# A block of stick-breaking attention beside a gated delta rule: the attention product with its scores as weights, fewer chains of reciprocal roots, and another order of projections and output

## The chip, the cores and the metric

One core of one Trainium2 chip runs the whole kernel in one launch. The metric is the device time of one execution in microseconds; it was taken three times for the kernel before, with a median of 704.29.

## What is computed

The reference is one decoder block on a sequence of 1024 tokens of width 1024. After an RMS norm, one input projection gives queries, keys, values and a gate for each of two groups of heads. Eight heads of 64 do strictly causal stick-breaking attention, four heads of 128 a gated delta rule in chunks. Each group is normed per head and gated with silu, both halves together go through the output projection, and the residual is added and normed.

```python
proj = jnp.einsum('btd,de->bte', h, w_in[layer])
sb_q, sb_k, sb_v, sb_z, g_q, g_k, g_v, g_z, g_b, g_a = jnp.split(proj, split_idx, axis=-1)
o_sb = stick_breaking_attention(...)   # A[t,s] = sigmoid(z_ts) * prod_{s<j<t} (1 - sigmoid(z_tj)); o = A v
o_sb = rmsnorm(o_sb.transpose(0, 2, 1, 3), sb_norm_w[layer]).reshape(b, t_len, SB_WIDTH) * jax.nn.silu(sb_z)
qkv = jax.nn.silu(causal_depthwise_conv(jnp.concatenate([g_q, g_k, g_v], axis=-1), gdn_conv_w[layer]))
gq, gk = l2norm(...), l2norm(...)
o_gdn = gated_delta_chunked(gq, gk, gv, decay, beta)   # S_t = exp(g) S (I - beta k k^T) + beta k v^T; o = S^T q
o_gdn = rmsnorm(o_gdn.transpose(0, 2, 1, 3), gdn_norm_w[layer]).reshape(b, t_len, GDN_WIDTH) * jax.nn.silu(g_z)
x = x + jnp.einsum('bte,ed->btd', jnp.concatenate([o_sb, o_gdn], axis=-1), w_out[layer])
return rmsnorm(x, final_norm_w)
```

## The kernel before

**Numbers in two parts.** The large products run in fp32r. An operand is split into a high part that fp32r holds and a low part, the rest; `mm3` (lines 514 to 517) makes a product of three matmuls from the two parts of each side. The scores of attention are split the same way into `ah` and `al`, while the values are kept with their high and low part side by side in `v2` (128 columns for a head of 64).

**Order.** The kernel does not fix its order by hand. Every piece of work is a generator (a `Stream`), and a model of the five engines (`Model`, lines 138 to 300) plays the program while it is recorded: an operation starts when its inputs are there by the model's costs, the streams take turns by priority, and the order that comes out is pinned on each engine as it stands. On TensorE the order is that in which the streams emit. One number of the model is how long TensorE needs at least between the starts of two matmuls, for the load of the weights (`op.columns`, line 169, used in line 285). The list `ORDER` (line 29) sets the order of the projections: `v0`, `v1` are the halves of the attention's values, `k0` to `k3` its keys, `z0` to `z7` the eight column blocks of the gates, `G0` to `G3` the query, key and value of a delta head. The projections are the filling: they go in where no other stream has work for TensorE (priority 100).

**Attention.** `window` (line 1125) treats two query blocks of 128 tokens at a time, so a head has four windows `w`. For each block, TensorE makes the logits in `z` (bank `pz`), ScalarE two sigmoids, VectorE the running product from the right (`cc`, a scan), Pool the product of both into `sg`. Then, in steps `j`, TensorE transposes the score blocks, ScalarE rounds them to `ah`, VectorE subtracts for `al`, and lines 1181 to 1185 multiply: the stationary operand (the weights) is the block `v2[:, s, :]`, the moving one `ah` or `al` with the columns of both query blocks, 256, or 128 where the key block is the last. The result `ov` (bank `po`) is transposed, so ScalarE copies it to `o2`, TensorE transposes that twice, VectorE adds the high and the low half in `oe`, and a DMA stores it in `o_s`. At most `WINDOWS` = 3 windows are in flight.

**Delta rule.** A head has two halves `g` of four chunks of 128 tokens. `gdn_pre` (line 879) transposes keys and queries, squares them with a sum, and runs a chain of a reciprocal root by Newton steps on VectorE (`_rsqrt`, 10 instructions on 8 numbers a row) for each of the eight halves; `gdn_inv` inverts the triangular matrices by blocks; `gdn_chain` runs the recurrence and ends with another such chain on 4 numbers a row (lines 1085 to 1091).

**Output.** `mixed` loads block `b` of 128 tokens of both groups from DRAM and norms it; `prepare` transposes it, applies the gates and splits it into `mh` and `ml`; `product` does 48 matmuls of 512 columns a block with the weights of the output projection, in the order of the eight row blocks `k`: 0 to 3 belong to attention, 4 to 7 to the delta rule. `out_weights` loads and splits those rows (`wo_split`: ScalarE makes `woh`, VectorE `wol`), 0 to 3 when the delta rule has ended, 4 to 7 when the projections have ended, since their place is that of the projections' input.

Of the kernel before, what the change touches and what calls it, by code (L numbers as in the profile page):

```python
# [10 lines left out]
F32 = mybir.dt.float32  # L11
# [6 lines left out]
P = 128  # L18
# [10 lines left out]
ORDER = "v0 v1 G0 k0 G1 z0 G2 k1 G3 k2 z1 z2 k3 z3 z4 z5 z6 z7".split()  # L29
WINDOWS = 3  # L30
# [72 lines left out]
class Pool:  # L103
# [6 lines left out]
    def tile(self, shape, dtype, name, tag=None, bufs=1):  # L110
# [7 lines left out]
        if len(slots) == bufs:  # L118
            old = next((r for r in slots if r.idle(self.ck.now)), slots[0])
            slots.remove(old)  # L120
            before += old.ops
# [16 lines left out]
class Model:  # L138
# [141 lines left out]
    def pull(self):  # L280
        if self.pe and not self.pe_busy and not self.pe[0].waits:
# [3 lines left out]
            at = max(self.now, op.ready, self.pe_began + 0.834 * op.columns)  # L285
# [107 lines left out]
def interleave(ck, room, streams):  # L393

    while streams:
        now = []
        if not ck.pe:
            free = room()
            now = [s for s in streams if (free or s.prio >= 100) and s.ready(ck)]
# [23 lines left out]
def block(tc, xT_d, x_d, n1_d, wE_d, wQ_d, wC_d, conv_d, alog_d, dtb_d, mixw_d, wo_d, fnw_d, out_d):  # L423
# [4 lines left out]
    with ExitStack() as top:  # L428
# [36 lines left out]
        rsg = cst.tile([P, GH, NB], F32, name="rsg")  # L465
        gsc = {n: cst.tile([P, GH, NB], F32, name=n) for n in ("beta", "cum", "eg", "neg", "egl", "kd")}
# [5 lines left out]
        o_s = dr.tile([NB, P, 512], F32, name="o_s")  # L472
# [55 lines left out]
        for tag, bufs in (("kh", 1), ("kl", 1), ("q2", 1), ("v2a", 2), ("v2a", 2), ("cc", 2), ("cc", 2), ("sg3", 1)):  # L528
            chl.append(at_.tile([P, 2, 520], F32R, tag=tag, bufs=bufs, name="chl"))
        sm = at_.tile([P, 768], F32, tag="sg2", name="sm")  # L530
# [95 lines left out]
        busy = {"w0": 0, "w1": 0, "w2": 0, "w3": 0, "T": 0, "al": 0, "po": 0, "inv": 0}  # L626
# [3 lines left out]
        def values(part):  # L630
            cs = slice(264 * part, 264 + 256 * part)
            n = 264 - 8 * part
            for b in range(NB):
                if part == 0 and 4 < b < 7:
                    row_scale(b - 5, dgs)
                if part == 0 and 4 <= b < 6:
                    dgp = at_.tile([P, 2, 256], F32, tag="sg0", name="dg")
                    dgs = [diagonal(dgp, 2 * (b - 4) + g) for g in range(2)]
# [16 lines left out]
        def decays(me):  # L655
# [41 lines left out]
            for h in range(GH):  # L697
                for g in range(2):
                    hc = slice(4 * g, 4 * g + 4)
                    dt = gd.tile([P, 4, P], F32, tag=("kn", "at", "nkv")[(2 * h + g) % 3], bufs=3, name="dt")  # L700
# [27 lines left out]
        def z_evac(i):  # L728
            def evac(pt, half):
# [9 lines left out]
                return S.dma_start(gate_s[i, :, hs], zt)  # L739
# [37 lines left out]
        def projections():  # L777
# [8 lines left out]
            def take():  # L786
                for n, (name, ok) in enumerate(todo):
                    if ok():
# [4 lines left out]
                        e = 4 + 4 * int(name[2]) + int(name[1]) if name[0] == "G" else e + int(name[1])  # L793
# [57 lines left out]
        def delta_pre():  # L851
            yield lambda: "v0" in flags
            yield from decays(pre)
            for h in range(GH):
                for g in range(2):
# [13 lines left out]
        def delta_scan():  # L869
            for h in range(GH):  # L870
                for g in range(2):
# [4 lines left out]
                    flags[f"c{u}"] = True  # L876
            flags["g"] = True

        def gdn_pre(h, g):
            st = gst[h, g] = {}  # L880
            kq, vt = gst[h]["kq"][g], gst[h]["vt"]
            cs = slice(4 * g, 4 * g + 4)
            kn = gd.tile([P, 4, P], F32, tag="kn", bufs=3, name="kn")
            ss = gd.tile([P, 2, 4], F32, tag="ss", name="ss")
# [4 lines left out]

            nkv = gd.tile([P, 4, P], F32, tag="nkv", bufs=3, name="nkv")  # L890
            for which in range(2):
                tp = pz()
                for j in range(4):
                    TE.transpose(tp[:, j * P:(j + 1) * P], kq[:, j, which, :], ident)
                for j in range(4):
                    A.activation(nkv[:, j, :], tp[:, j * P:(j + 1) * P], AF.Square, accum_out=ss[:, which, j:j + 1])
                sq = [("A", 250)] * 4
                if which == 0:
                    V.tensor_copy(kn.rearrange("p c d -> p (c d)"), tp)
                    yield  # L900
            V.tensor_scalar(ss, ss, EPS, None, ALU.add)
            rr = gd.tile([P, 2, 4], F32, tag="rr", bufs=3, name="rr")
            _rsqrt(V, gd, rr.rearrange("p a c -> p (a c)"), ss.rearrange("p a c -> p (a c)"), 8, "rru")
            r2b = gd.tile([P, 4], F32, tag="r2b", bufs=3, name="r2b")
            V.tensor_tensor(r2b, rr[:, 0, :], rr[:, 0, :], ALU.mult)
            V.tensor_tensor(r2b, r2b, gsc["beta"][:, h, cs], ALU.mult)
            mr2b = gd.tile([P, 4], F32, tag="mr2b", name="mr2b")
            r = V.tensor_scalar(mr2b, r2b, -1.0, None, ALU.mult)
            nk = gd.tile([P, 4], F32, tag="nk", name="nk")
            V.tensor_tensor(nk, ss[:, 0, :], rr[:, 0, :], ALU.mult)  # L910
            r2k = gd.tile([P, 4], F32, tag="r2k", bufs=3, name="r2k")
            V.tensor_tensor(r2k, r2b, gsc["kd"][:, h, cs], ALU.mult)
            yield r
            nm = dt
            at = gd.tile([P, 4, P], F32, tag="at", bufs=3, name="at")
# [12 lines left out]
            st.update(kn=kn, rr=rr, r2b=r2b, r2k=r2k, nkv=nkv, nm=nm, at=at)  # L928
# [10 lines left out]
        def gdn_inv(h, g):  # L939
# [45 lines left out]
            V.tensor_copy(W[0:32, :, 0:32], wc[0:32])  # L985
            V.tensor_copy(W[32:64, :, 32:64], wc[32:64])
# [24 lines left out]
            for q in range(2):  # L1011
                o = 64 * q
                V.tensor_copy(X[o:o + 32, :, o + 32:o + 64], xv[o:o + 32])
# [16 lines left out]
        def gdn_chain(h, g):  # L1030
            st = gst[h, g]
            kq, kn, nkv, at = gst[h]["kq"][g], st["kn"], st["nkv"], st["at"]
            r2b, r2k, rr = st["r2b"], st["r2k"], st["rr"]
# [369 lines left out]
```

## Time and profile before

| | |
|---|---|
| Time, median of 3 runs (lowest to highest) | 704.29 us (703.46 to 705.93) |
| The profiled execution, its own time | 705.37 us |
| Its span in the profile | 703.7 us |
| Granted TensorE clock, mean | 0.989 |
| DMA | 96.42 MB, 137 GB/s on average |

The profile's page has the busy time of each engine (PE is TensorE, PEld its weight loads, DVE VectorE, ACT ScalarE, POOL GpSimd, SP the queue of the DMAs), the span in slices, and the chain of work that ended last: from the last instruction back to what released it, step by step. The groups gather instructions of one kind; since every operation is recorded through one helper, all have the line L315, and groups are told apart by the tiles that they write and read (`po<-ah,v2a` writes `po` and reads `ah` and `v2a`). A duration in the groups runs from an instruction's start to its end; matmuls overlap, so the step from start to start is shorter.

### The profile page before, as it was taken

Reading aid. Unit: us, or ns where it says so; the run is one execution under the profiler, and the core shown is the slowest. Engines: PE = TensorE matmul, PEld = TensorE weight load, DVE = VectorE, ACT = ScalarE, POOL = GpSimd, SP = SyncE. Lnnn points to the kernel's source line nnn. Section 1 sums busy time; section 2 is a strip of 40 time slices with the busy share of each in tenths; the row PEclk is TensorE's granted clock in tenths of the full one; section 3 lists DMA queues with packets and bytes.
Section 4 is the critical chain, followed back from the end, with each engine's and each line's share of the span. In section 5 each row is a group of like instructions: output and inputs, shape, how many; then the busy total and the mean of one; then the engine's idle time right before and its main releaser. Section 6 shows DMA issues by size and latency. Waiting matters only on the chain.

```text
span 703.7 us, 12998 instructions
## 1 busy us (share of the span) xinstructions
PE 680.7 (97%) x4510; PEld 575.7 (82%) x4510; DVE 544.7 (77%) x1463; ACT 363.4 (52%) x885; POOL 263.9 (38%) x223
## 2 busy tenths in 40 slices
PE   8999999999899999999999999999999999889995
PEld 6889998887677888878888888888788888678885
DVE  5364525668898987898999999897787987997843
ACT  5661248436567543675856677643377853311212
POOL 0000147545352523442344442454335455443221
PEclk9999999999899999999999999999999999999998
DMA  8936364271142236224235051333524366645321
GB/s 300 370 121 255 112 223 162 90 260 32 49 139 75 69 97 206 71 70 141 72 109 169 12 173 42 109 96 105 174 65 153 98 225 225 217 145 181 113 94 61
DMA packets 76498, 96.42 MB, mean 137 GB/s; under 512 B 24656, under 2 KB 45712, under 8 KB 76432
## 3 DMA queue, kind: packets, MB, share of 16 engines
q1 hardware_dynamic: 76432, 95.58, 42.1%
q8 instruction: 36, 0.59, 0.4%
q14 instruction: 30, 0.25, 0.1%
HBM read 67.67 MB, written 27.89 MB: 136 GB/s over the span
## 4 chain that ended last, share of the span: by engine, by line
PE 86%; DVE 7%; issue 2%; ACT 2%; DMA 1%; SPq 0%; POOLq 0%; POOL 0%; DVEq 0%
PE pp L315 55%; PE pz L315 23%; PE po L315 5%; PE pc L315 3%; DVE cc L315 2%; DMA xr<-xT 1%; DVE pp L315 1%; ACT sg L315 1%; DVE y L315 0%; DVE al L315 0%; ACT pz L315 0%; DVE tm L315 0%; DVE wol L315 0%; DMA xc<-xd 0%; ACT xinv L315 0%
## 5 line engine op out<-in xcount | busy, mean ns | idle before, releaser
L315 PE MATMUL pp<-xh,weh 128*128 128x512 f32 x384 | 161.0, 419 | 0.5 <-DVE ac L315 0.5
L315 PE MATMUL pp<-xh,wel 128*128 128x512 f32 x384 | 151.2, 394 | 0.0
L315 PE MATMUL pp<-xl,weh 128*128 128x512 f32 x384 | 150.7, 393 | 0.0
L315 POOL TENSOR_TENSOR sg<-sg,cc 128x128 f32<-128x128 f32 (+3 forms) x64 | 77.3, 1209 | 114.7 <-DVE cc L315 74.5
L315 POOL TENSOR_TENSOR wel<-wer,weh 128x512 fp32r<-128x512 f32 x48 | 62.9, 1313 | 85.2 <-ACT weh L315 82.3
L315 PEld LDWEIGHTS pp<-xh,wel 128*128 128x128 f32 x384 | 72.4, 188 | 16.2
L315 PEld LDWEIGHTS pp<-xh,weh 128*128 128x128 f32 x384 | 72.6, 189 | 12.3 <-DVE ac L315 1.1
L315 PEld LDWEIGHTS pp<-xl,weh 128*128 128x128 f32 x384 | 72.8, 190 | 10.2
L315 ACT ACTIVATE sg<-pz,rs 128x384 f32<-128x384 f32 (+3 forms) x96 | 53.1, 586 | 18.5 <-PE pz L315 17.8
L315 ACT ACTIVATE ah<-pz 128x512 fp32r<-128x512 f32 (+1 forms) x80 | 43.7, 558 | 29.6 <-PE pz L315 28.8
L315 DVE TENSOR_TENSOR_SCAN cc<-pz,step 128x384 f32<-128x384 f32 (+2 forms) x64 | 53.9, 847 | 2.8 <-ACT pz L315 2.4
L315 PE MATMUL pp<-wol,mh 128*128 128x512 f32 (+1 forms) x136 | 52.1, 383 | 1.3 <-DVE wol L315 1.3
L315 DVE TENSOR_TENSOR al<-pz,ah 128x512 fp32r<-128x512 f32 (+1 forms) x80 | 49.9, 629 | 3.6 <-ACT ah L315 3.3
L315 PE MATMUL pp<-woh,mh 128*128 128x512 f32 (+1 forms) x136 | 52.6, 387 | 0.0
L315 PE MATMUL pp<-woh,ml 128*128 128x512 f32 (+1 forms) x136 | 52.0, 382 | 0.6 <-POOL ml L315 0.6
L315 ACT ACTIVATE pz<-pz,ns 128x384 f32<-128x384 f32 (+3 forms) x96 | 52.0, 564 | 0.1
L315 PE MATMUL pz<-step,sg 128*128 128x128 f32 x288 | 45.3, 281 | 3.7 <-DVE oe L315 2.4
L315 PE MATMUL pp<-chl,xh 128*128 128x264 f32 (+1 forms) x256 | 46.8, 284 | 0.0
L315 DVE TENSOR_TENSOR tm<-xs,br 128x8 f32<-128x8 f32 (+14 forms) x120 | 45.0, 375 | 0.9
L315 DVE SCALAR_TENSOR_TENSOR pp<-pre,conv,pp 128x512 f32<-128x512 f32 x48 | 36.0, 751 | 8.7 <-ACT pp L315 8.4
L315 POOL TENSOR_TENSOR ml<-mf,mh 128x512 fp32r<-128x512 f32 x16 | 24.5, 1536 | 48.2 <-ACT mh L315 47.0
L315 PE MATMUL po<-ah,v2a 128*128 128x256 f32 (+1 forms) x160 | 42.3, 288 | 0.0
(234 smaller groups left out, 1613.5 us busy)
## 6 DMA issues: line engine op xcount, KB each, us to landing
wer<-wE SPq DMA_DIRECT2D x48, 256.0 KB, 3.6
xr<-x SPq DMA_DIRECT2D x16, 512.0 KB, 6.2
qk_s<-xq SPq DMA_DIRECT2D x8, 512.0 KB, 4.7
v_s<-v2e SPq DMA_DIRECT2D x16, 256.0 KB, 2.0
q<-qk_s SPq DMA_DIRECT2D x8, 512.0 KB, 4.2
v2a<-v_s SPq DMA_DIRECT2D x8, 512.0 KB, 7.2
kh<-qk_s SPq DMA_DIRECT2D x8, 512.0 KB, 4.6
kl<-qk_s SPq DMA_DIRECT2D x8, 512.0 KB, 6.1
```

The lines of the kernel that those rows point to most:

```text
L315: ins = f(*args, **kw).ins
```

## The change

1. **The attention product.** A window is one query block `b` (eight a head, up to six in flight). The stationary operand is now a 128x128 block of `ah` or `al`, the moving one `v2[:, k, :]`, 128 columns. The result is not transposed; ScalarE copies it from `po` to `oe` and a DMA stores its high and low half apart in `o_s`. The two halves are added by Pool in `mixed`. The copy `o2`, its transposes and the reduction on VectorE go.
2. **The model** takes 0.42 ns a column for the load of fp32r weights and 0.834 for others, where it took 0.834 for all.
3. **Chains.** `gdn_norms` does the norms of both halves of a head at once: four chains on 16 numbers a row instead of eight on 8. The chain at the end of `gdn_chain` becomes one for all heads, on 32 numbers a row, when the last head has ended. The copies into `kn`, `W` and part of `X` move from VectorE to ScalarE.
4. **Projections.** `v1` comes after `k0`, `z1` after `k3`, and the gates are numbered so that `z0` to `z3` are the delta rule's.
5. **Output.** The weight rows 4 to 7 are loaded and split first, during attention. `mixed_delta` prepares the delta rule's half of a block alone, ahead of `mixed`; the product takes the halves in the order (0, delta), (1, delta), (0, attention), (1, attention), and from block 2 on the delta rule's rows first.

```diff
-ORDER = "v0 v1 G0 k0 G1 z0 G2 k1 G3 k2 z1 z2 k3 z3 z4 z5 z6 z7".split()
-WINDOWS = 3
+ORDER = "v0 G0 k0 v1 G1 z0 G2 k1 G3 k2 k3 z1 z2 z3 z4 z5 z6 z7".split()
+WINDOWS = 6
...
-            op.columns = int(np.prod(inputs[0].shape[1:]))
+            op.load = int(np.prod(inputs[0].shape[1:])) * (0.42 if inputs[0].dtype == F32R else 0.834)
...
+        def gdn_norms(h):
+
+            ss = gd.tile([P, 2, NB], F32, tag="ss", name="ss")
...
+                    if which == 0:
+                        A.activation(kns[g].rearrange("p c d -> p (c d)"), tp, AF.Copy)
+
+                    for j in range(4):
+                        js = tp[:, j * P:(j + 1) * P]
+                        A.activation(js, js, AF.Square, accum_out=ss[:, which, 4 * g + j:4 * g + j + 1])
+                    yield
+            V.tensor_scalar(ss, ss, EPS, None, ALU.add)
+            rr = rkq[:, h]
+            _rsqrt(V, gd, rr.rearrange("p a c -> p (a c)"), ss.rearrange("p a c -> p (a c)"), 2 * NB, "rru")
...
-            V.tensor_copy(W[0:32, :, 0:32], wc[0:32])
-            V.tensor_copy(W[32:64, :, 32:64], wc[32:64])
+            A.activation(W[0:32, :, 0:32], wc[0:32], AF.Copy)
+            A.activation(W[32:64, :, 32:64], wc[32:64], AF.Copy)
...
-            _rsqrt(V, gd, t0, sso, 4, "t0u")
-            V.scalar_tensor_tensor(rsg[:, h, 4 * g:4 * g + 4], rq, P ** -0.5, t0, ALU.mult, ALU.mult)
...
-                for s in (2 * (j - 1), 2 * (j - 1) + 1):
-                    i0 = 0 if s <= 2 * w else 1
-                    c = slice(256 * (s % 2), 256 * (s % 2) + (1 if i0 else 2) * P)
-                    for m, t in enumerate((ah, al)):
-                        TE.matmul(ov[:, i0 * P:256], v2[:, s, :], t[:, c], start=(s == 0 and m == 0), stop=(s == 2 * w + 1 and m == 1))
+                for u in range(n):
+                    k = 4 * (j - 1) + u
+                    for t in (ah, al):
+                        TE.matmul(ov, t[:, u * P:(u + 1) * P], v2[:, k, :], start=(k == 0 and t is ah), stop=(k == b and t is al))
...
-            o2 = at_.tile([P, 256], F32, tag="o2", name="o2")
-            yield A.activation(o2, ov[:, 0:256], AF.Copy)
+            oe = at_.tile([P, P], F32, tag="oe", bufs=3, name="oe")
+            yield A.activation(oe, ov, AF.Copy)
             busy["po"] = 0
-            op = pz()
-            for i in range(2):
-                TE.transpose(op[:, i * P:(i + 1) * P], o2[:, i * P:(i + 1) * P], ident)
-            oe = at_.tile([P, 2, SBD], F32, tag="oe", bufs=2, name="oe")
-            V.tensor_reduce(oe, op[:, 0:256].rearrange("p (i u d) -> p i d u", i=2, u=2), AX.X, ALU.add)
-            flags[f"e{h}{w}"] = S.dma_start(o_s[2 * w:2 * w + 2, :, h * SBD:(h + 1) * SBD].rearrange("b t d -> t b d"), oe)
+            flags[f"e{h}{b}"] = S.dma_start(o_s[b, :, :, h * SBD:(h + 1) * SBD].rearrange("u t d -> t u d"), oe.rearrange("p (u d) -> p u d", u=2))
...
-            for k in range(4):
+            for k in range(4, NK):
                 yield wo_raw(k)
                 wo_split(k)
             flags["wo"] = True
...
+                S.dma_start(mx[:, 0:512], o_s[b, 0])
+                sq = fi.tile([P, 512], F32, tag="sq", name="sq")
+                S.dma_start(sq, o_s[b, 1])
+                gate6(b)
+                G.tensor_tensor(mx[:, 0:512], mx[:, 0:512], sq, ALU.add)
+                G.tensor_tensor(sq, mx[:, 0:512], mx[:, 0:512], ALU.mult)
...
+        def halves():
+            return [(0, 1), (1, 1), (0, 0), (1, 0)] + [(b, g) for b in range(2, NB) for g in (1, 0)]
...
+                ks = [4, 5, 6, 7, 0, 1, 2, 3]
+                if b < 2:
+                    ks = ks[0:4] if half else ks[4:8]
```

The same place on TensorE in both orders, an attention product in the middle of a head. `po<-ah,v2a` is a matmul of AV; the size is that of its result (partitions x columns). Before:

```order
L315 MATMUL po<-ah,v2a 128x256
L315 MATMUL po<-al,v2a 128x256
L315 MATMUL po<-ah,v2a 128x128
L315 MATMUL po<-al,v2a 128x128
L315 MATMUL pz<-kh,q_2098 128x512
L315 MATMUL pz<-kl,q_2098 128x512
L315 MATMUL pz<-wc,dt 32x32 x16
L315 MATMUL pz<-step,o_2247 128x128 x2
```

Now, in two pieces, the beginning and the end of one group. `po<-v2a,ah` is a matmul that moves `v2` past a block of `ah`; `pc<-xct` and `pz<-v_2445,kn` are the delta rule's:

```order
L316 MATMUL pp<-xh,weh 128x512
L316 MATMUL pp<-xl,weh 128x512
L316 MATMUL pp<-xh,wel 128x512
L316 MATMUL pc<-xct,xinv_537 128x128
L316 MATMUL po<-v2a,ah 128x128
L316 MATMUL po<-v2a,al 128x128
```

The end of the group, and what follows it on TensorE:

```order
L316 MATMUL po<-v2a,ah 128x128
L316 MATMUL po<-v2a,al 128x128
L316 MATMUL pz<-v_2445,kn 128x128
L316 MATMUL pz<-step,sg 128x128 x4
L316 MATMUL pp<-xh,weh 128x512
```

Between these two pieces the pair of `ah` and `al` repeats: 14 matmuls of 128 columns stand in a row, where two or three wider pairs and one narrow one stood; the transposes of `o` are gone, and the results of AV have 128 columns each.

On VectorE, at the end of the projections. `zt<-pp` is the last gate's evacuation, `wol` the split of a row block of output weights, `mf` the gated half of an output block, `ssb` and `rsb` the norm of the next. Before:

```order
L315 TENSOR_TENSOR zt<-pp,rbc 128x512
L315 SCALAR_TENSOR_TENSOR wol_7646<-wor,mixw,woh_7645 128x1024
L315 SCALAR_TENSOR_TENSOR wol_7650<-wor,mixw,woh_7649 128x1024
L315 TENSOR_TENSOR mf<-pz,gt 128x384
L315 TENSOR_TENSOR mf<-pz,zt 128x128
L315 TENSOR_TENSOR mf<-pz,gt 128x512
L315 TENSOR_REDUCE ssb<-sq 128x8
L315 TENSOR_SCALAR ssb<-ssb 128x8
L315 TENSOR_SCALAR rsb<-ssb 128x8
L315 SCALAR_TENSOR_TENSOR wol_7654<-wor,mixw,woh_7653 128x1024
L315 SCALAR_TENSOR_TENSOR wol_7658<-wor,mixw,woh_7657 128x1024
```

Now:

```order
L316 TENSOR_TENSOR mx<-mx,rsb 128x512
L316 TENSOR_TENSOR zt<-pp,rbc 128x512
L316 TENSOR_TENSOR mf<-pz,gt 128x384
L316 SCALAR_TENSOR_TENSOR wol_7783<-wor,mixw,woh_7782 128x1024
L316 SCALAR_TENSOR_TENSOR wol_7787<-wor,mixw,woh_7786 128x1024
L316 SCALAR_TENSOR_TENSOR wol_7791<-wor,mixw,woh_7790 128x1024
L316 SCALAR_TENSOR_TENSOR wol_7795<-wor,mixw,woh_7794 128x1024
L316 TENSOR_TENSOR mf<-pz,zt 128x128
L316 TENSOR_SCALAR mx<-mx,rsg 128x128 x4
```

The four splits of the last rows stand together, ahead of the last quarter of block 0's attention half (`mf<-pz,zt`); the rows that were split here earlier, 0 to 3 of the old order, are split as 4 to 7 further up, between the scans of attention.

More of the change, by code (lines that the diff above doesn't have):

```diff
@@ L118, in tile @@
         if len(slots) == bufs:
-            old = next((r for r in slots if r.idle(self.ck.now)), slots[0])
+            old = slots[0] if turn else next((r for r in slots if r.idle(self.ck.now)), slots[0])
             slots.remove(old)
@@ L284, in pull @@
             self.begin(op)
-            at = max(self.now, op.ready, self.pe_began + 0.834 * op.columns)
+            at = max(self.now, op.ready, self.pe_began + op.load)
             self.pe_began = at
@@ L398, in interleave @@
             free = room()
-            now = [s for s in streams if (free or s.prio >= 100) and s.ready(ck)]
+            now = [s for s in streams if (free or s.prio >= 100 or s.prio < 0) and s.ready(ck)]
         if not now:
@@ L625, in block @@
         gst = {}
-        busy = {"w0": 0, "w1": 0, "w2": 0, "w3": 0, "T": 0, "al": 0, "po": 0, "inv": 0}
+        busy = {**{f"w{b}": 0 for b in range(NB)}, "T": 0, "al": 0, "po": 0, "inv": 0}
         def values(part):
@@ L888, in gdn_pre @@
             S.dma_start(dt, dt_s[h, g])
[L890 to L913, printed above, removed]
+            nkv = gd.tile([P, 4, P], F32, tag="nkv", bufs=3, turn=True, name="nkv")
             nm = dt
-            at = gd.tile([P, 4, P], F32, tag="at", bufs=3, name="at")
+            at = gd.tile([P, 4, P], F32, tag="at", bufs=3, turn=True, name="at")
             for i in range(2):
@@ L1226, in out_weights @@
             flags["wo"] = True
-            yield lambda: f"s{SBH - 1}3" in flags
-            for k in (4, 5):
+            yield lambda: f"s{SBH - 1}{NB - 1}" in flags
+            for k in (0, 1):
+                wo_raw(k)
+            flags["late"] = True
+            yield lambda: f"e{SBH - 1}{NB - 1}" in flags
+            for k in (2, 3):
                 wo_raw(k)
@@ L1232, in out_weights @@
             pools[1] = open_pool("f1", before=px.ops(), side="right")
-            for k in (6, 7):
-                wo_raw(k)
+            for k in range(4):
+                wo_split(k)
             fnw = wts["fnw"] = pools[1].tile([P, D], F32, name="fnw")
@@ L1312, in product @@
+                A.activation(hv, fv, AF.Copy)
+                ready[b, g] = G.tensor_tensor(lv, fv, hv.bitcast(F32), ALU.subtract)
+                yield
+        def product():
+            ys = {}
+            for b, half in halves():
+                if b > 1 and half:
+                    continue
+                yield lambda: (b, half) in ready
+                yield ready[b, half]
+                mh, ml, xr = ready[b]
                 last = b == NB - 1
                 parts = [slice(0, 512), slice(512, 768), slice(768, D)] if last else [slice(0, 512), slice(512, D)]
-                steps = [(g, n, k) for g in range(2) for n in range(len(parts)) for k in range(4 * g, 4 * g + 4)]
@@ L1326, in product @@
+                if b < 2:
+                    ks = ks[0:4] if half else ks[4:8]
+                if not half:
+                    yield lambda: "fnw" in flags
+                    y = pools[1].tile([P, D], F32, tag="y", bufs=2, name="y")
+                    sy = pools[1].tile([P, 3], F32, tag="sy", bufs=2, name="sy")
+                for n, k in [(n, k) for n in range(len(parts)) for k in ks]:
+                    if k < 4 and b == 0:
                         yield wts[k][2]
-                    if k == 0:
-                        yield lambda: ps.room("pp", 2)
```

289 lines of the change are left out of this document (149 added, 140 removed).

## The prediction

> **What bounds the kernel now.** I read the page first: its head, the busy line and the chain that ended last.
>
> ```profile
> span 703.7 us, 12998 instructions
> PE 680.7 (97%) x4510; PEld 575.7 (82%) x4510; DVE 544.7 (77%) x1463; ACT 363.4 (52%) x885; POOL 263.9 (38%) x223
> PE 86%; DVE 7%; issue 2%; ACT 2%; DMA 1%; SPq 0%; POOLq 0%; POOL 0%; DVEq 0%
> ```
>
> TensorE is busy for 680.7 of 703.7 us and makes up 86% of the chain that ends last; 23.0 us are left in which it is idle. A busy matmul row is no measure of what a matmul costs, though: the matmuls overlap, and the mean of one in the groups is longer than the step from one start to the next. I took the steps from two other views: the chain in order of time, near the end, where TensorE waits for nothing (start, length, what, count), and the table by windows (length, then busy time and count of each engine), in the value projections, which are all of 256 or 264 moving columns.
>
> ```profile
> 649.32 0.87 PE pz L315 x8
> 650.19 11.07 PE pp L315 x48
> 60.00:100.00 40.00, 40.00 (x332) 39.78 (x331) 17.70 (x57) 9.44 (x22) 6.44 (x9) 1.00 0.41 146
> ```
>
> So a matmul of 512 columns in fp32r costs 11.07 / 48 = 0.231 us of TensorE, one of 256 columns 40.00 / 332 = 0.120, a 128x128 transpose 0.87 / 8 = 0.109. The kernel is a queue of such steps on one engine in a fixed order. Where the queue stands still is seen in the windows, whose first column of busy time is PE's.
>
> ```profile
> 0.00:25.00 25.00, 22.82 (x93) 18.05 (x94) 14.11 (x17) 14.03 (x17) 0.70 (x6) 1.00 0.89 322
> 150.00:200.00 50.00, 44.59 (x219) 36.51 (x218) 42.80 (x106) 28.82 (x71) 21.33 (x19) 0.93 0.37 114
> 350.00:400.00 50.00, 49.80 (x367) 41.37 (x366) 48.54 (x138) 30.80 (x68) 24.25 (x20) 1.00 0.33 101
> 600.00:620.00 20.00, 17.66 (x77) 13.13 (x76) 18.81 (x47) 5.71 (x9) 9.11 (x7) 1.00 0.63 207
> 620.00:640.00 20.00, 17.70 (x80) 14.49 (x79) 17.64 (x67) 3.98 (x7) 6.96 (x6) 0.91 0.46 138
> 680.00:704.00 24.00, 16.32 (x95) 14.15 (x93) 7.91 (x27) 4.25 (x10) 4.06 (x4) 0.89 0.17 66
> ```
>
> Of the 23.0 us idle, 2.2 lie at the start and 7.7 in the last window; neither end's code changes. The 13.1 between them are what a better order can win: 5.4 where attention begins (150 to 200), 4.6 where the projections end and the output begins (600 to 640), 3.1 elsewhere. VectorE at 48.5 of 50 us (350 to 400) costs TensorE only 0.2 there.
>
> **AV, the largest term.** These are the groups by form (busy, mean ns of one), for their counts:
>
> ```profile
> L315 PE MATMUL po<-ah,v2a 128*128 128x256 f32 x128 | 36.5, 305 | 0.0
> L315 PE MATMUL po<-al,v2a 128*128 128x256 f32 x128 | 33.9, 285 | 0.0
> L315 PE MATMUL po<-al,v2a 128*128 128x128 f32 x32 | 8.8, 275 | 0.0
> L315 PE MATMUL po<-ah,v2a 128*128 128x128 f32 x32 | 7.1, 222 | 0.0
> L315 PE MATMUL pz<-step,o 128*128 128x128 f32 x64 | 12.6, 278 | 1.3 <-DVE xs L315 1.0 <-DVE t0u L315 0.3
> ```
>
> In their place come 8 heads x 36 blocks x 2 (high and low part) = 576 matmuls, each with its own 128x128 block of `ah` or `al` as weights and 128 columns of `v2` moving; the 64 transposes of `o2` go. What does a matmul of 128 moving columns cost when each brings new weights? Here is the timeline of TensorE (start, length) and then of its weight loads, at 205 us, where two such matmuls stand between longer ones:
>
> ```profile
> 204.88 0.22 PE L315 MATMUL po<-ah,v2a 128*128 128x128 f32 x1
> 204.94 0.28 PE L315 MATMUL po<-al,v2a 128*128 128x128 f32 x1
> 205.06 0.44 PE L315 MATMUL pz<-kh,q 128*128 128x512 f32 x1
> 205.34 0.40 PE L315 MATMUL pz<-kl,q 128*128 128x512 f32 x1
> ```
>
> ```profile
> 204.88 0.19 PEld L315 LDWEIGHTS po<-al,v2a 128*128 128x128 f32 x1
> 205.00 0.19 PEld L315 LDWEIGHTS pz<-kh,q 128*128 128x128 f32 x1
> 205.11 0.19 PEld L315 LDWEIGHTS pz<-kl,q 128*128 128x128 f32 x1
> ```
>
> The 0.06 us between the starts at 204.88 and 204.94 is the tempting number, since the stream itself is that short. But from 204.88 to 205.34 stand the two 128s and one matmul of 512: 0.46 - 0.231 = 0.229 us for the pair, 0.115 each. The loads say why: they start 0.12 and 0.11 apart, though all are fp32r, and nothing else held them. A load of 128 columns of fp32r weights takes 0.11 us, hides behind a matmul of 256 columns (0.120), and does not hide behind one of 128.
>
> Now the sum. Before: 256 x 0.120 + 64 x 0.115 + 64 x 0.109 = 30.7 + 7.4 + 7.0 = 45.1 us. After: 576 x 0.112 (between the transpose's step of 0.109 and the pair's 0.115) = 64.5 us, +19.4. The first load of each of the 8 x 12 = 96 groups (per head four query blocks with one group, four with two) can run under the longer matmul ahead of it, which saves at most 96 x 0.05 = 4.8, so +14.6. I take +16. The ends are -10.5 (576 x 0.060 = 34.6, if new weights came as fast as the stream) and +21.1 (576 x 0.115 = 66.2 and nothing hidden).
>
> The Trainium skill ("TensorE: Matmul & The Clock Gate", Back-to-back issue gap) gives about 81 ns per matmul for a sustained stream of load and matmul pairs at 128 columns; by that the new AV would be an estimated 576 x 0.081 = 46.7 us and this term +1.6. The trace's pair at 0.115 each speaks against it.
>
> **Waits that go with the transposes of `o2`.** Timeline, at the first heavy head:
>
> ```profile
> 180.06 0.39 PE L315 MATMUL pz<-kl,q 128*128 128x512 f32 x1
> 181.43 0.41 PE L315 MATMUL pz<-step,o 128*128 128x128 f32 x2 [0.98 <-DVE xs L315]
> 184.26 1.09 PE L315 MATMUL pz<-step,sg 128*128 128x128 f32 x4 [2.42 <-DVE oe L315]
> ```
>
> Between 180.06 and 184.26 TensorE has work for 0.231 + 2 x 0.109 = 0.45 us, so 3.7 us are lost, 2.6 of them to the bank that VectorE's reduction into `oe` frees. Now ScalarE evacuates `po` straight to `oe`. The transposes of `sg` can still wait on VectorE's other work there: 0 to -3.7, I take -3.
>
> **The start of the output.** Timeline at 600 us, and one row of the chain:
>
> ```profile
> 600.60 0.40 PE L315 MATMUL pp<-wol,mh 128*128 128x512 f32 x1
> 601.61 0.51 PE L315 MATMUL pp<-woh,ml 128*128 128x512 f32 x1 [0.62 <-POOL ml L315]
> 602.65 0.39 PE L315 MATMUL pp<-woh,mh 128*128 128x512 f32 x1
> 604.08 0.50 PE L315 MATMUL pp<-wol,mh 128*128 128x512 f32 x1 [1.05 <-DVE wol L315]
> 621.46 2.29 issue
> ```
>
> Here 0.8 us go to a half of block 0 that was not ready, 1.2 to the split of a weight row, 2.3 to block 1's. In the new order the delta rule's four weight rows are split during attention, and the 48 matmuls of the first two delta halves (48 x 0.231 = 11.1 us) stand between the last projection and the first use of the other four rows. Those four splits take VectorE
>
> ```profile
> L315 DVE SCALAR_TENSOR_TENSOR wol<-wor,mixw,woh 128x1024 fp32r<-128x1024 f32 x8 | 12.2, 1538 | 2.6 <-ACT woh L315 2.6
> ```
>
> 4 x 1.54 = 6.2 us, so they are covered with 4.9 us to spare; were that cover gone, they would cost up to 6.2. What is late next is the attention half of blocks 0 and 1, which stands behind these splits in VectorE's order. 0 to -4.6 (the idle time of 600 to 640); I take -4.
>
> **VectorE.** The groups by form whose counts shrink or move:
>
> ```profile
> L315 DVE TENSOR_REDUCE oe<-pz 128x128 f32<-128x256 f32 x32 | 13.3, 414 | 2.9 <-PE pz L315 2.8
> L315 DVE SCALAR_TENSOR_TENSOR rr<-rru,rr 128x8 f32<-128x8 f32 x24 | 10.3, 427 | 0.3
> L315 DVE SCALAR_TENSOR_TENSOR t0u<-t 128x4 f32<-128x4 f32 x24 | 6.4, 265 | 0.2
> L315 DVE SCALAR_TENSOR_TENSOR t<-t0u,t 128x4 f32<-128x4 f32 x24 | 5.2, 218 | 0.1
> L315 DVE COPY w<-wc 32x128 f32<-32x128 f32 x16 | 6.2, 388 | 0.1
> ```
>
> The reduction goes (-13.3); `rr`'s row halves to 12 (-5.2); the two rows of the output's chain fall from 24 to 3 (-10.2); the copies into `w` move to ScalarE (-6.2). That is -35 us of 544.7, and the chains' other steps and the copies into `kn` and `xinv` go with them; ScalarE, 52% busy, has room. Against it stand 16 more, smaller subtractions into `al`. TensorE does not wait for VectorE's sum, only where an input is late; of the 3.1 us idle outside the two places above and of what the start of attention loses beyond the 3.7, I count -4 (0 to -6), partly because a TensorE that falls behind finds its inputs ready. For waits that I do not see in the old trace (single-block windows, 16 AV matmuls in a row ahead of the delta rule's short ones, `o_s` written in 64 DMAs instead of 32 and read in two halves, a Pool addition per block ahead of the squares) I add 1 (0 to +8).
>
> **Sum.** The profiled run took 705.37 us, its span 703.7. 705.4 + 16 - 3 - 4 - 4 + 1 = 711.4. It lay 1.1 above the median of the runs, 704.29, so I give 710 on that scale: slower by 0.8%. About 0.3%, 2.1 us, is what a measurement of this kernel can tell from no change.
>
> **Rivals.** *Fast loads.* If blocks of `ah` and `al` load as fast as 128 columns stream, AV costs 34.6, its term is -10.5, and with the other terms' -10 the time is 704.3 - 10.5 - 10 = 684. For it speaks that some loads are shorter than others:
>
> ```profile
> L315 PEld LDWEIGHTS pz<-step,sg 128*128 128x128 f32 x288 | 33.7, 143 | 7.6 <-issue 3.1 <-DVE dt L315 0.8 <-POOL sg L315 0.7
> L315 PEld LDWEIGHTS po<-al,v2a 128*128 128x128 f32 x160 | 30.5, 191 | 1.9 <-DVE al L315 0.4
> ```
>
> The loads of transposes take 143 ns; those of AV take 191, and they are fp32r already. New is only which of the two fp32r operands is loaded, so I give it 0.12. The Trainium skill ("TensorE: Matmul & The Clock Gate", Weight-path perf modes) says that the fast weight load is on for 128 weights of any type but FP32; by that fp32r could be the short kind, and these rows show it long. *In between:* loads that overlap in part in a long run of pairs, as two 128s in a row never do here, at halfway between 0.060 and 0.112: 576 x 0.086 = 49.5, +4.4, time 704.3 + 4.4 - 10 = 699. It gets 0.06. *All waits gone.* If the lighter VectorE and the new order remove the 13.1 us idle and the 4 or so that the busy rows hide (3.7 lost against 3.4 idle at 180), the time is 704.3 + 16 - 17 = 703, no change; it decides from about 14 us of waits removed. The two places named hold 10 of the 13, which is for it; that each new order has waits of its own is against. It gets 0.16. *New waits.* The attention halves of blocks 0 and 1 stand behind the four splits on VectorE; if they come late, neither place is won and TensorE waits up to the 8 that I allowed: 704.3 + 16 - 4 + 8 = 724. It gets 0.05. The forecast itself has 0.61.
>
> **How the numbers follow.** The forecast's own spread is +14.6 to +21.1 for AV and -14 to +1 for the rest, 705 to 726 at its corners, which are seldom met together. To hold 8 in 10 the range takes in the waits-gone and the in-between case and leaves out the fast loads, the upper corner and the new waits: 695 to 721. Faster by over 0.3%: fast loads 0.12, in-between 0.06, a third of waits-gone 0.05, 0.02 of the forecast: 0.25. Within 0.3%: the rest of waits-gone and 0.04 of the forecast: 0.15. Slower: 0.60.
>
> **What would show it.** In the new trace, AV's weight loads start 0.11 us apart in groups of 8 and 16 rows, and the 576 matmuls take about 61 to 65 us; no row `pz<-step,o` and no wait for `oe` on VectorE; no wait for `wol` after the last projection; VectorE between 485 and 510 us busy. Loads 0.06 apart would make the forecast wrong by the first rival; idle time of TensorE under 12 us with loads at 0.11, by the third.

## The result

The changed kernel took 710.85 us (median of 4 runs, 709.81 to 711.42), the kernel before, beside it, 703.95 (703.46 to 705.93): a ratio of 1.0091 with a 95% interval of 1.0067 to 1.0115. The forecast was 710. The medians differ by 6.9 us; the two profiled runs, 709.81 and 705.37, differ by 4.4, and the sums of the next section are of that pair.

### The profile page after: what moved, and what is told of

Its sections match the earlier page's. It is cut to its first block, busy times and chain, and to the rows that moved or that the text cites. A ratio compares the mean times of both kernels' runs of the same rounds, so it can differ in the third digit from the quotient of the medians.

```text
span 708.1 us, 13405 instructions
## 1 busy us (share of the span) xinstructions
PE 691.6 (98%) x4702; PEld 590.1 (83%) x4702; DVE 516.1 (73%) x1245; ACT 383.7 (54%) x975; POOL 270.2 (38%) x231
## 5 line engine op out<-in xcount | busy, mean ns | idle before, releaser
L316 PE MATMUL po<-v2a,al 128*128 128x128 f32 x288 | 68.3, 275 | 0.0
L316 PE MATMUL po<-v2a,ah 128*128 128x128 f32 x288 | 67.3, 271 | 0.0
L316 DVE TENSOR_TENSOR al<-pz,ah 128x512 fp32r<-128x512 f32 (+2 forms) x96 | 51.7, 549 | 19.9 <-ACT ah L316 19.4
L316 PEld LDWEIGHTS po<-v2a,ah 128*128 128x128 f32 x288 | 55.0, 191 | 2.2
L316 PEld LDWEIGHTS po<-v2a,al 128*128 128x128 f32 x288 | 55.1, 191 | 2.0 <-DVE al L316 0.2
L316 ACT ACTIVATE ah<-pz 128x512 fp32r<-128x512 f32 (+2 forms) x96 | 45.4, 493 | 9.9 <-PE pz L316 9.2
L316 DVE TENSOR_TENSOR tm<-xs,br 128x8 f32<-128x8 f32 (+14 forms) x120 | 47.6, 397 | 2.2
L316 PE MATMUL pp<-woh,mh 128*128 128x512 f32 (+1 forms) x120 | 46.4, 387 | 0.0
L316 PE MATMUL pp<-woh,ml 128*128 128x512 f32 (+1 forms) x120 | 45.3, 378 | 0.0
```

What stands on the lines that cost most here:

```text
L316: ins = f(*args, **kw).ins
```

## The profile after, beside the one before

The page's head and busy line of the changed kernel:

```profile
span 708.1 us, 13405 instructions
...
PE 691.6 (98%) x4702; PEld 590.1 (83%) x4702; DVE 516.1 (73%) x1245; ACT 383.7 (54%) x975; POOL 270.2 (38%) x231
```

TensorE is busy 10.9 us longer and idle 6.5 us less (16.5 against 23.0): +4.4 in all. But a busy microsecond isn't always worth the same. The view of cores gives the mean clock that TensorE was granted, first of the kernel before:

```profile
core 0: 703.7 us, clock 0.989
```

and of the changed one:

```profile
core 0: 708.1 us, clock 0.996
```

0.011 x 703.7 = 7.7 us of full speed were missing before, 0.004 x 708.1 = 2.8 are missing now. Of these, 2.6 and 2.8 fall into the last window of each run, behind TensorE's last matmul, where they slow no work. So the work itself, at full clock, went from about 675.6 (680.7 - 5.1) to 691.6 us: **about +16**; idle time gave back 6.5, the clock 5.1. Part of the clock's share belongs to this pair of runs: in 39 other runs of the kernel before, the clock was 0.992 to 0.995 (median 0.993, or 4.9 us missing), and two of the four runs of the changed kernel had 0.992. By the medians, which differ by 6.9, some 9 us came back beside the +16, not 11.6. The windows of the changed kernel (length, then PE busy first; the clock is the third number from the end) show where:

```profile
0.00:25.00 25.00, 23.04 (x94) 18.20 (x95) 14.39 (x18) 14.27 (x17) 0.70 (x6) 1.00 0.91 327
150.00:200.00 50.00, 49.93 (x448) 41.78 (x447) 43.45 (x107) 31.30 (x77) 18.50 (x15) 1.00 0.45 137
...
600.00:620.00 20.00, 20.00 (x93) 16.37 (x92) 17.10 (x37) 6.06 (x7) 6.95 (x7) 1.00 0.63 197
620.00:640.00 20.00, 17.87 (x86) 14.13 (x85) 18.85 (x55) 4.61 (x8) 9.22 (x7) 1.00 0.55 168
680.00:708.10 28.10, 20.23 (x114) 17.33 (x112) 11.96 (x36) 4.25 (x10) 5.25 (x5) 0.90 0.14 57
```

At the start of attention (150 to 200) idle time went from 5.4 to 0.1 us and the clock from 0.93 to 1.00, worth 3.5 more: 8.8 together. At the handover (600 to 640) idle time went from 4.6 to 2.1 and the clock of the second half from 0.91 to 1.00 (1.8): 4.3. What is left of waiting is in the table of TensorE's waits (us in total, times, longest). Before, it had these two rows:

```profile
PE pz L315 <- DVE oe L315: 2.9, 2, 2.4
...
PE pp L315 <- DVE wol L315: 1.3, 2, 1.0
```

and now:

```profile
PE pz L316 <- DVE mx L316: 2.0, 1, 2.0
PE pp L316 <- DVE kt L316: 1.5, 1, 1.5
...
PE pz L316 <- DVE cc L316: 0.8, 4, 0.3
...
PE pz L316 <- ACT oe L316: 0.4, 1, 0.4
```

The waits for `oe` on VectorE and for `wol` are gone. New are `mx`, the attention half of block 3 at 637.8, and `kt`, where a projection waits at 120 us until VectorE has evacuated a block of keys. What brings `kt` is not shown: `e7q_order` below, which has the new orders alone, doesn't wait for it.

The added work is AV. Weight loads of one group of it, from the timeline of TensorE's loads (start, length):

```profile
457.00 0.19 PEld L316 LDWEIGHTS po<-v2a,al 128*128 128x128 f32 x1
457.11 0.19 PEld L316 LDWEIGHTS po<-v2a,ah 128*128 128x128 f32 x1
457.22 0.19 PEld L316 LDWEIGHTS po<-v2a,al 128*128 128x128 f32 x1
457.33 0.19 PEld L316 LDWEIGHTS po<-v2a,ah 128*128 128x128 f32 x1
457.45 0.19 PEld L316 LDWEIGHTS po<-v2a,al 128*128 128x128 f32 x1
```

Each starts 0.11 us after the one before, as the loads at 204.88 did in the old trace. Added up over TensorE's whole timeline, from the start of each AV matmul to the start of the next matmul, less idle time, the 576 take 64.2 us, 0.111 each. The old AV with the transposes of `o2` took 45.8 by the same count, so AV's own rows grew by 18.4. All of TensorE's work grew by about 2.4 less than that; which other rows became cheaper was not taken apart.

## Experiments

Three questions were open: what a load really costs, whether AV's price is the whole loss, and which part brings the gain. "Price" below is the planner's cost of a weight load, 0.834 ns a column before, 0.42 for fp32r in the changed kernel. Every ratio is to the kernel before, timed beside. The edits are shortened: `...` and the comments stand for what is left out.

### The load by itself

The whole block is replaced by runs of TensorE alone: 64 matmuls of one kind in a row, with 16 of 512 columns between most of the kinds. A row of the list has the name, the weights, the moving operand, the columns of the weights, the moving columns, and the number of blocks of weights taken in turn.

```diff
+stages = (("warm", wr, mr, P, 512, 8), ("each128", wr, mr, P, 128, 8), ("mid", ...),
+          ("same128", wr, mr, P, 128, 1), ("mid2", ...), ("each256", wr, mr, P, 256, 8),
+          ("bf128", wb, mb, P, 128, 8), ("mid3", ...), ("half64", wr, mr, 64, 128, 8))
```

> Only TensorE rows are computed here, not the block: runs of 64 matmuls with 128 moving columns, weights that change each time (fp32r, 128 columns), the same fp32r weights each time, weights of 64 columns, bf16 weights and moving data, and for comparison 256 moving columns. Load theory: the step from start to start is 0.109 to 0.112 us with 128 columns of fp32r weights, whether they change or not (0.115 in the pair of the old trace), about 0.06 with 64 columns of weights, 0.12 with 256 moving columns. Fast-load rival: 0.06 with fp32r weights of 128 columns. Run-overlap rival: about 0.086. Bf16 weights are not in the old trace; no theory needs them.

The chain in order of time (start, length, what, count); `each` is fp32r with new weights for each matmul, first with 128, then with 256 moving columns, `same` with the same weights again and again, `bf` with bf16 operands, `half` fp32r with weights of 64 columns:

```profile
22.10 7.09 PE each L41 x64
29.19 3.74 PE mid L41 x16
32.93 7.10 PE same L41 x64
...
43.76 7.67 PE each L41 x64
51.43 3.59 PE bf L41 x64
...
58.73 3.85 PE half L41 x64
```

128 moving columns in fp32r cost 7.09 / 64 = 0.111 us, 256 cost 0.120, 512 cost 3.74 / 16 = 0.234. With half the weight columns the step of the same 128 moving columns nearly halves, to 0.060. So in fp32r it is the load that is paid, by its columns; and it is paid for the same weights too (0.111), since every matmul is issued with its load (64 loads for 64 matmuls of `same`). In bf16 the step is 0.056; there weights and moving data both changed, so that what sets it is not separated. The rival of fast loads and the one in between fall here.

### AV taken back out, and the planner's price

`e1_rest` is the changed kernel with attention's windows and AV as before (`v2` as weights, transposes of `o2`); `e1p_rest_model` is the same, planned by the old price; `e4_model` is the changed kernel planned by the old price. To make room, the two blocks of a window share one tile without padding, and `oe` has one buffer, in the first two.

```diff
-for u in range(n):
-    k = 4 * (j - 1) + u
-    for t in (ah, al):
-        TE.matmul(ov, t[:, u * P:(u + 1) * P], v2[:, k, :], ...)
+for s in (2 * (j - 1), 2 * (j - 1) + 1):
+    for m, t in enumerate((ah, al)):
+        TE.matmul(ov[:, i0 * P:256], v2[:, s, :], t[:, c], ...)
```

```diff
-op.load = int(np.prod(inputs[0].shape[1:])) * (0.42 if inputs[0].dtype == F32R else 0.834)
+op.load = int(np.prod(inputs[0].shape[1:])) * 0.834
```

> The change without its first part: attention with v2 as weights, two blocks a window, transposes of o2, as before; chains, projections' order and output as after. Load theory: AV's 16 us go and what the rest gains stays, so 710.9 - 16 = 695 (691 to 699). Rival A, the AV matmuls cost little and the new order of streams is what costs: 704 to 711. Rival B, the gain came from the missing transposes of o2 and their waits, and the rest gains nothing: 704.

> The version with attention as before and the rest of the change, planned with a weight load of 0.834 ns per column. If the price hardly matters, 695 to 699, as the same version planned with 0.42 for fp32r (697.4). If the true price lets the planner find a better order, below 695; if the order that 0.42 gave was a lucky one, 700 to 704.

> The changed kernel with the planner's price of a weight load back at 0.834 ns per column for all weights, the price by which the kernel before was planned; nothing else differs but the order that comes out. Since a fp32r load was measured at 0.110 us per 128 columns, 0.42 prices it at half, and the planner takes the new AV for 35 us cheaper than it is. If the planner's wrong price is part of the loss, this order gives 705 to 708. If the loss is AV's matmuls alone, it stays within 3 us of 711.

`e1_rest` took 697.43 us, 0.9926 (0.9911 to 0.9942); `e1p_rest_model` 695.00, 0.9898 (0.9878 to 0.9918); `e4_model` 715.77, 1.0188 (1.0163 to 1.0214), outside both of its expectations. So the rest of the change gains 5 to 7 us without the new AV, and both of these versions beat the kernel before and the changed one. By the ratios AV costs 0.0165 x 704 = 11.6 us at the price 0.42 and 0.0290 x 702 = 20.4 at 0.834. In the timelines, counted as above, its rows take 64.2 us against 45.3 in `e1_rest`, and 65.8 in `e4_model` against 44.5 in `e1p_rest_model`: about 19 and 21 of work. How the plans turn these into 11.6 and 20.4 was not taken apart. The price near the measured one (0.111 us for 128 columns is 0.87 ns a column, so 0.834) gives the worse plan for the changed kernel, by 6.8 us, and, if anything, the better one without its AV (2 us, with intervals that touch): a plan is worth some us either way, and whether its costs are right doesn't tell which.

### The low part of the scores left out

`e5_no_low` doesn't make AV's 288 matmuls of `al`; `e5f_same_plan` doesn't either, but the planner counts them, so all else stays in the changed kernel's order.

```diff
-for t in (ah, al):
-    TE.matmul(ov, t[:, u * P:(u + 1) * P], v2[:, k, :], start=(k == 0 and t is ah), stop=(k == b and t is al))
+TE.matmul(ov, ah[:, u * P:(u + 1) * P], v2[:, k, :], start=(k == 0), stop=(k == b))
```

```diff
+if t is al:
+    ck.record("P", None, [ov], list(args[1:]), cost("P", "matmul", args, {}), None)
+else:
+    TE.matmul(*args, start=(k == 0), stop=(k == b))
```

> The changed kernel without the 288 matmuls of the low part of the scores (al) in AV; the output lacks that part. Load theory: each of them holds TensorE for 0.110 us, so 31.7 us go, and with the waits that appear behind a shorter stream (0 to 4 us) it comes to 679 to 683. If loads were hidden in the stream of 128 columns (0.06 each), 17 us go: 694. If AV were beside the path, the time would stay within 3 us of 711.

> The changed kernel without the 288 matmuls of the low part of the scores, as in the run e5_no_low (the output lacks that part), but the planner still counts them, so that the other engines' order and TensorE's remaining order are those of the changed kernel. Load theory: 288 x 0.110 = 31.7 us go from TensorE, and it comes to 679 to 684 us with a little new waiting behind the shorter stream. If the loads were hidden (0.06 each), 694. If the end is set by the other engines and not by TensorE, as e5_no_low's 715 could also be read, it stays above 700.

`e5_no_low` missed every expectation: 714.97 us, 1.0177 (1.0147 to 1.0207), with 31.7 us less work than the changed kernel. With the plan kept, 689.96, 0.9819 (0.9795 to 0.9843): by the ratios 0.0272 x 704 = 19.1 us gone, less than the load theory's 27 to 32, more than the 17 of hidden loads and not far from them, so that the time alone doesn't decide between the two. The trace does: by the same count AV's 288 remaining matmuls take 32.2 us, so 32.0 of the 64.2 are gone, 0.111 for each one left out. The profile shows part of what came back: the span shrank by 22.8, TensorE is busy 26.7 less (664.9) and idle 3.9 more (20.4). Where the other 5 of the 32 came back among the busy rows is not shown. That the end is set elsewhere than on TensorE, the third reading, falls with the kept plan. In the run that was planned anew the stream runs dry at the handover:

```profile
PE pz L316 <- DMA mx<-o_s: 9.0, 1, 9.0
PE pz L316 <- DVE mx L316: 7.7, 4, 3.5
```

`o_s` is attention's half, which is fetched right behind the delta half. Attention itself is not later there: its last result leaves at 557.0, against 558.3 with the plan kept, where the waits for `mx` come to 1.8. What comes late is told by the transfers of the delta rule's results to DRAM and back (count, durations in ns, first and last start in us). In the run planned anew:

```profile
L316 SPq DMA_DIRECT2D og_s<-goe x32: 319/327/970, 193.6 to 551.4; - x32
L316 SPq DMA_DIRECT2D mx<-og_s x8: 320/456/978, 580.3 to 648.5; - x8
```

and with the plan kept:

```profile
L316 SPq DMA_DIRECT2D og_s<-goe x32: 319/332/812, 194.2 to 504.9; - x32
L316 SPq DMA_DIRECT2D mx<-og_s x8: 319/453/525, 541.1 to 628.8; - x8
```

The same instructions in another order: the delta rule ends 46 us later, the output's first inputs are fetched 39 us later, and 25 us are lost. The two rows of waits hold 16.7 of them; the rest was not taken apart.

### Each part alone

`e6_chains` is the kernel before with the delta rule's shorter chains alone (with the unpadded tiles and one `oe`), `e7_order` with the new order of projections and output alone, `e2_av` with AV block by block alone. All three take the delta rule's buffers strictly in turn, as the changed kernel does (the list of the change doesn't name it); `e7_order` and `e2_av` are planned by the price 0.42.

```diff
+yield from gdn_norms(h)     # e6_chains: one chain for a head, squares on ScalarE, one chain for the output
```

```diff
-ORDER = "v0 v1 G0 k0 G1 z0 G2 k1 G3 k2 z1 z2 k3 z3 z4 z5 z6 z7".split()
+ORDER = "v0 G0 k0 v1 G1 z0 G2 k1 G3 k2 k3 z1 z2 z3 z4 z5 z6 z7".split()     # e7_order, with mixed_delta, prepare and product by halves
```

```diff
-TE.matmul(ov[:, i0 * P:256], v2[:, s, :], t[:, c], ...)
+TE.matmul(ov, t[:, u * P:(u + 1) * P], v2[:, k, :], ...)     # e2_av, with one block to a window and o_s in two halves
```

> The third part alone on the kernel before: four and one chains of reciprocal roots instead of eight and eight, copies into kn, W and X on ScalarE. Theory that VectorE's relief counts: 700 (698 to 702). Rival, that VectorE is not on the path and the gain lies in the output's order: 704 (703 to 706).

> The kernel before with the new order of projections and of the output alone: attention, AV and the delta rule's chains stay as before. If the two orders are what gains (the attention halves, the weight splits and the squares no longer waited for at the handover), it comes to 697 to 700 us, close to the 697.4 of the version that has the chains as well. If the shorter chains carry part of the gain, as the prediction's term of -4 for VectorE has it, it comes to 701 to 702. If the new order needs the lighter VectorE to work at all, it comes to 703 or more.

> The first two parts of the change alone on the kernel before: AV block by block with ah and al as weights, one block a window, no transposes of o2, the model's 0.42. Load theory: 704 + 16 to 17 for the matmuls, less 0 to 4 for the waits at the transposes of o2: 716 to 721. Rival A: below 711, since the matmuls cost little. Rival B: 704 + 16 - 10 = 710.

All three came out slower than the kernel before. `e6_chains`: 705.93 us, 1.0047 (1.0028 to 1.0065), although VectorE is busy 502.5 us in place of 544.7. `e7_order`: 717.37, 1.0215 (1.0191 to 1.0239). `e2_av`: 736.91, 1.0491 (1.0470 to 1.0511), 16 us above the top of what was expected. Before believing the last two, the buffers and the price had to be ruled out. `e9_turn` is the kernel before with only the buffers in turn; `e7q_order` and `e2q_av` repeat the two with the old price and the old choice of buffers.

```diff
-old = next((r for r in slots if r.idle(self.ck.now)), slots[0])
+old = slots[0] if turn else next((r for r in slots if r.idle(self.ck.now)), slots[0])
```

> The kernel before with one thing changed: the delta rule's buffers are taken strictly in turn, as in the changed kernel, in place of any that the planner sees idle. If that rule is what cost e2_av and e7_order their extra 10 to 20 us, it comes to 712 to 720. If it is harmless, 702 to 706.

> The kernel before with the new order of projections and of the output alone, as e7_order, but planned with the old price of a weight load and with the delta rule's buffers taken as before, not strictly in turn. If e7_order's 717 came from these two, it comes to 697 to 702. If the new orders need the delta rule's shorter chains, it stays at 710 or more.

> The kernel before with AV block by block alone, as e2_av, but planned with the old price of a weight load (0.834 ns per column) and with the delta rule's buffers taken as before, not strictly in turn. If e2_av's 737 came from the price or from the buffers taken in turn, it comes to 716 to 721, AV's own +13 to +16. If the block by block AV really doesn't go with the old output's order, it stays at 730 or more.

`e9_turn`: 702.41 us, 0.9993 (0.9981 to 1.0004), harmless. `e7q_order`: 720.64, 1.0254 (1.0228 to 1.0281), and `e2q_av`: 742.77, 1.0577 (1.0540 to 1.0614), both no better than their first form. So the parts alone cost 0.5, 2.5 and 5.8%, and together 0.9%. Each of these runs is planned anew, and a new plan alone moved the time by 2 to 25 us above, so the sizes of the parts alone are uncertain by as much. The traces show one way in which they need each other. First the delta rule's transfers of the kernel before:

```profile
L315 SPq DMA_DIRECT2D og_s<-goe x32: 319/320/459, 229.7 to 545.4; - x32
L315 SPq DMA_DIRECT2D mx<-og_s x8: 422/467/872, 561.8 to 643.3; - x8
```

with the shorter chains alone (`e6_chains`):

```profile
L315 SPq DMA_DIRECT2D og_s<-goe x32: 319/332/1265, 233.3 to 516.5; - x32
L315 SPq DMA_DIRECT2D mx<-og_s x8: 320/496/866, 561.4 to 645.2; - x8
```

with the new order alone (`e7q_order`):

```profile
L316 SPq DMA_DIRECT2D og_s<-goe x32: 319/326/537, 189.1 to 543.9; - x32
L316 SPq DMA_DIRECT2D mx<-og_s x8: 319/440/559, 586.9 to 658.8; - x8
```

and with both (`e1p_rest_model`):

```profile
L316 SPq DMA_DIRECT2D og_s<-goe x32: 319/328/615, 191.4 to 501.7; - x32
L316 SPq DMA_DIRECT2D mx<-og_s x8: 320/428/629, 539.4 to 634.6; - x8
```

The chains let the delta rule end 29 us sooner (516.5 against 545.4; with the buffers in turn alone, in `e9_turn`, it is 544.9), and the old output doesn't use it: it fetches that half at 561, with the attention half. The new output fetches the delta half as soon as its weights are split, some 40 us behind the delta rule's end; with the long chains that is 586.9, right before the projections run out, with the short ones 539.4. What it costs to be late stands in `e7q_order`'s timeline of TensorE around the first product of the output (idle time and its releaser in brackets):

```profile
597.51 0.60 PE L316 MATMUL pz<-step,mx 128*128 128x128 f32 x4
602.54 0.80 PE L316 MATMUL pp<-woh,mh 128*128 128x512 f32 x1 [4.44 <-ACT mh L316]
603.14 0.63 PE L316 MATMUL pp<-wol,mh 128*128 128x512 f32 x1
...
604.70 0.63 PE L316 MATMUL pp<-woh,mh 128*128 128x512 f32 x1
605.12 0.63 PE L316 MATMUL pp<-wol,mh 128*128 128x512 f32 x1
605.55 0.63 PE L316 MATMUL pp<-woh,ml 128*128 128x512 f32 x1
...
608.89 0.40 PE L316 MATMUL pp<-wol,mh 128*128 128x512 f32 x1
609.12 0.40 PE L316 MATMUL pp<-woh,ml 128*128 128x512 f32 x1
```

and in ScalarE's:

```profile
597.71 4.26 ACT L316 ACTIVATE woh<-wor,mixw 128x1024 fp32r<-128x1024 f32 x4 [3.97 <-PE pp L316]
601.88 0.61 ACT L316 ACTIVATE mh<-mf 128x512 fp32r<-128x512 f32 x1
```

The late delta half queues behind the four splits that the last projection sets free. With a second wait for `mh`, at 622, that is the first row of `e7q_order`'s waits:

```profile
PE pp L316 <- ACT mh L316: 7.2, 2, 4.4
```

The handover is not the largest loss of `e7q_order`, though. From 600 to 640 it costs 5.6 us more than in the kernel before (idle 6.8 against 4.6, and 5.2 against 1.8 by the clock). From 350 to 400 it costs 10.6 more, against the row of the kernel before that the prediction shows (49.80 busy at 1.00):

```profile
350.00:400.00 50.00, 44.21 (x339) 35.88 (x337) 45.31 (x111) 29.38 (x70) 18.06 (x14) 0.90 0.33 101
```

The longest wait there, 1.7 us, is for `ac` on VectorE, which is busy 9.5 of the 10 us from 350 to 360, while TensorE is busy 6.4. With the chains as well (`e1p_rest_model`) TensorE is busy 49.3 of these 50 us at 1.00. So the lighter VectorE may count there beside the earlier end of the delta rule; no run separates the two.

In `e2q_av` the old output needs the attention half first, attention's last result leaves at 606.3 in place of 577.9, and TensorE waits for `mx` three times at the output, from 644 us on:

```profile
PE pz L315 <- DVE mx L315: 8.0, 3, 5.6
```

That is a third of what `e2q_av` loses beyond AV's own 16. That attention's later end makes these waits is argued, not shown, and where the rest comes from stays open.

## Why the prediction was right, and where it was not

**AV, +16: right.** All of TensorE's work grew by about 16 us at full clock, loads stand 0.11 apart, and the load by itself measures 0.111. The sum behind the term held too: AV's rows take 64.2 us now (64.5 in the prediction) and took 45.8 before (45.1). The first rival (fast loads) and the second (in between) are refuted by the load's own run. By the figure of the Trainium skill that the prediction cited ("TensorE: Matmul & The Clock Gate", Back-to-back issue gap), 81 ns a matmul, the term would have been an estimated +1.6; the load's own run measures 111 ns for fp32r.

**The waits of the transposes, the output's start, VectorE and new waits, -3 - 4 - 4 + 1 = -10: right in sum, and in part by luck.** The profiled pair gave 11.6 (6.5 of idle time, 5.1 of the clock), the medians about 9, and `e1_rest` and `e1p_rest_model` gain 5 to 7 where the terms without -3 said 7. By place, in the profiled pair: 8.8 at the start of attention, 4.3 at the handover, and elsewhere between the two ends 1.3 us more idle time than before (4.4 against 3.1).

**What failed: what the three gains were put down to.** The step "waits that go with the transposes of `o2`" names the wrong part. With the transposes gone but the old order of projections (`e2q_av`), and with the transposes kept but the new order (`e7q_order`), the start of attention reads:

```profile
150.00:200.00 50.00, 44.66 (x246) 37.62 (x245) 41.61 (x106) 31.47 (x82) 21.76 (x19) 0.97 0.41 122
150.00:200.00 50.00, 49.05 (x455) 40.25 (x454) 43.17 (x112) 31.02 (x71) 19.85 (x16) 1.00 0.39 120
```

All runs with the old order idle there for 4.3 to 5.4 us, with either form of AV; all with the new orders for 0.1 to 1.1. Without the reduction the wait for `oe` goes, and waits for `cc`, `ac` and `al` on VectorE stand in its place. So the gain there comes with the new orders; which of their edits brings it was not separated.

The step "VectorE", that a lighter VectorE is worth -4 where inputs are late, isn't borne out as a term by itself: with 42 us less of VectorE `e6_chains` is no faster. What the chains bring that the traces show is the delta rule's earlier end, and only the new output makes use of it. The step "the start of the output", that the new order is worth -4 by itself, fails too: alone, the new orders lose 17 us (`e7q_order`), 5.6 of them at the handover, where the prediction had a gain. It costed the cover of the splits (11.1 us of delta halves) as given, but that stands only if those halves are there before the projections end, which the chains decide. It named the price of a lost cover, 6.2; `e7q_order` waited 4.4 behind the four splits and lost about 3 more to the clock.

**What lay hidden in the busy rows: the clock.** The prediction put what the old trace could give back at 13.1 us of idle time and 4 or so hidden in busy rows, without saying by what. At the two places that were won it was the clock, 5.3 in the profiled pair. So "all waits gone" was nearer than its 703 looks: 11.6 of its 17 went in that pair, about 9 by the medians.

**Of the signs:** no transposes of `o2`, no wait for `oe` on VectorE or for `wol`, AV's loads 0.11 apart, its matmuls 64.2 us: as said. The groups are of 2 to 16 matmuls in a row, not of 8 and 16. VectorE between 485 and 510: no, 516.1; the durations of its rows fell by 52 us in sum, but its busy time only by 28.6, which was not taken apart. "What is late next", the attention halves of blocks 0 and 1: no, block 3's, by 2.0 us.

## What to carry to other kernels

Where TensorE's weights are fp32r, give each load at least 256 moving columns, or the load is the step (0.120 us against a load of 0.111; nothing between 128 and 256 columns was measured): choose as weights the operand that is reused over the wider side. Before adding up the terms of a change, ask which term is the condition of another; here three parts that lose alone lose far less together than their sum. And in a kernel whose order a planner makes, test a cost with the plan held still: the same instructions planned anew moved by 25 us, more than the change under study.

## What the runs showed of the hardware

**A wait can cost more than its length.** After the 4.44 us in `e7q_order`, matmuls of 512 columns start 0.43 us apart (604.70, 605.12, 605.55) and return to 0.23 only at 608.89: of the 6.35 us from 602.54, the 13 matmuls need 3.0 at full clock, and 0.3 is another wait. The row of that stretch in the windows has the granted clock:

```profile
605.00:610.00 5.00, 5.00 (x15) 3.87 (x15) 3.68 (x8) 0.00 (x0) 2.31 (x2) 0.62 0.30 104
```

The kernel before did the same behind its wait at 184:

```profile
184.00:188.00 4.00, 3.74 (x12) 3.07 (x13) 3.99 (x10) 1.12 (x2) 1.28 (x1) 0.50 0.32 86
188.00:192.00 4.00, 4.00 (x22) 3.74 (x21) 2.35 (x6) 1.75 (x4) 1.77 (x1) 0.76 0.28 71
```

TensorE counts as busy there, at half speed. The Trainium skill ("TensorE: Matmul & The Clock Gate", Part 1) has the array at half rate after an idle window of about 3.4 us and at full rate again after a busy one; the wait of 4.44 us and the slow 6 us behind it are of that order. In the traces' record of the clock the stretches at half rate last 3.41 us or a multiple of it: 6.83 behind this wait and behind the one at 184, and 3.41 behind the wait of 2.30 us at 621 in the kernel before. So the wait need not be as long as 3.4 us. Nor does its length alone decide: 2.47 us at 400 in `e7q_order` and 1.97 us at 637.8 in the changed kernel left the clock at 1.00.

**A fp32r load is paid even when the weights don't change**, 0.111 us for 128 columns. The step in bf16, with new weights each time, was 0.056.
